# A two-layer decoder trunk: query projection in 12 tiles, rope rows moved by DMA, cumulated steps and first scan later

## The chip, the cores and the metric

The program runs on one core of a Trainium2 chip. The metric is the device time of one execution in microseconds; the median of three runs of the kernel before is 1911.82 us (1910.69 to 1912.57). The engines are named as the profile names them: PE (TensorE matmuls; PEld its weight loads), DVE (VectorE), ACT (ScalarE), POOL (GpSimd) and SP (SyncE, which issues DMAs). Each engine works through its own queue in order; semaphores join the queues.

## What is computed

Two decoder layers over 512 positions of width 1024, in float32. Each has a mixer with a Mamba-2 scan (SSD) of 16 heads in 4 groups next to a latent attention of 16 heads, a cross attention into 256 memory tokens and a gated MLP. The part that the change touches, cut from the reference:

```python
proj = h @ w_in[i]
z, xbc, dt_raw, c_q, c_kv, k_rope = jnp.split(proj, IN_SPLITS, axis=-1)
dt = jax.nn.softplus(dt_raw + dt_bias[i])
a_cs = jnp.cumsum(dt * a)                          # per chunk of 128, for the scan
q = (rmsnorm(c_q, q_norm) @ w_uq).reshape(b, s, MLA_HEADS, QK_NOPE + QK_ROPE)
q_nope = q[..., :QK_NOPE]                          # 64 wide
q_pe = apply_rope(q[..., QK_NOPE:], cos, sin)      # 32 wide: t1*cos - t2*sin, t2*cos + t1*sin
k_pe = apply_rope(k_rope, cos, sin)
sc = q_nope @ k_nope.T + q_pe @ k_pe.T             # then mask, softmax, times v
```

## The kernel before

Activations lie transposed, 128 channels by 512 positions to a tile. A float32 product is made of three matmuls (mm3, L168 to L170): both operands are split into a rounded part and a rest, and high times high, low times high, and high times low are summed in PSUM. Weights arrive by SP's queue into two raw buffers (wraw, L99); ACT writes the rounded part (whi, L107) and POOL, for some tiles DVE, the rest (wlo, L108), each into one of three buffers. So a load waits until the split of the tile two loads ago is done, and a split waits until PE has used the tile three splits ago. PSUM has 8 banks.

The order on PE is that of the program text; a scheduler orders the other engines' queues. A layer starts with the latent tiles of the input projection (query, key and value latents, key rope, dt). Then a loop interleaves generators: `projections` gives 24 input projection tiles of 24 matmuls, six for each scan group (the convolution of the first four in a group is L480 to L491, done by DVE and ACT), then `attention_head`, then `attention` with its 16 heads. In each step of that loop the lead `front`, the side work `memory` and the scans `ssd` go one step further.

`front` rotates the key's rope part (L433 to L436), makes 1/rms of both latents (the transposes of L263 and the columns by L265 to L273), broadcasts them by PE (L280), scales the rope tables for the queries (L442, L443), normalises and splits the key/value latent (L448 to L452), and then makes the cumulated sums of the scan. PE does these in L455 and L456 from w, which DVE ends in L428, the last of the dt chain L413 to L428; DVE copies the sums (L457), PE transposes them (L465), and a DMA takes them to DRAM, from which the scans fetch rows (R).

`ssd(g)` fetches its rows, then has a heavy step (transposes, decays on ACT and POOL), an empty one, the states (L558 on PE, then DVE and ACT), and the outputs (L578; L584 needs the states, made by L567 and L569). The scans go at positions 6g + 4 and after, position 26 left out.

A head in `attention` has parts in the order SKVAMTQ: scores, keys, values, attend, a memory key tile, transposes, and the query tile of the head two further on. `queries` makes 9 matmuls for one head: its columns of w_uq hold 64 plain rows, 32 rope rows and the same 32 with halves swapped; DVE multiplies the tile by a table of ones, cosines and sines, scaled by the query's 1/rms (L661), and ACT and DVE split it (L159, L162). After attention come 8 tiles of memory values; each of these steps ends with `mixed`, which writes operands of the output projection (split by L165).

Of the kernel before, what the change touches and what calls it, by code (L numbers as in the profile page):

```python
# [12 lines left out]
F32 = mybir.dt.float32  # L13
# [41 lines left out]


@with_exitstack
def trunk(ctx: ExitStack, tc: tile.TileContext, t: dict, out: bass.AP):
# [26 lines left out]
    MEM_AT = (3, 5, 7, 9, 11, 13, 14, 15)  # L85
    specs = []
# [120 lines left out]
    G.memset(mhalf, -0.5)  # L207

# [9 lines left out]
    csa = cp.tile([P, S], F32, name="csa")  # L218
    csb = cp.tile([P, S], F32, name="csb")
# [8 lines left out]
    def prepare():  # L228
        V.tensor_scalar(half[:, :, 0:80], small[:, :, o_cw:o_cw + 80], 0.5, None, ALU.mult)
        V.tensor_scalar(half[:, :, 80:], small[:, :, o_sn:o_sn + KD], 0.5, None, ALU.mult)  # L230

        ang, rnd, tab = unit(), unit(), unit()
# [3 lines left out]
        V.tensor_scalar(rnd, ang, 1.0 / (2 * math.pi), rc[:, 1:2], ALU.mult, ALU.add)  # L236
        V.tensor_scalar(rnd, rnd, magic, None, ALU.add)
# [6 lines left out]
        phs = cp.tile([P, 1], F32, name="phs")  # L244
        V.tensor_scalar(phs, rc[:, 1:2], 2 * math.pi, None, ALU.mult)
        V.tensor_scalar(ang, ang, phs, None, ALU.add)
        V.tensor_scalar(ang, ang, 3.1415925, -3.1415925, ALU.min, ALU.max)
        A.activation(tab, ang, AF.Sin)
        V.tensor_scalar(tab, tab, rc[:, 2:3], None, ALU.mult)
        G.memset(csa[0:64], 1.0)  # L250
        V.tensor_copy(csa[64:128], tab[64:128])
        V.tensor_copy(csb[0:64], tab[0:64])
        G.memset(csb[64:128], 1.0)
        A.activation(nega, small[:, :, o_al:o_al + HEADS], AF.Exp)
        V.tensor_scalar(nega, nega, -1.0, None, ALU.mult)
# [105 lines left out]
    for layer in range(L):  # L361

        cqh, cql, cqs = [], [], Squares()
# [11 lines left out]
        csqa, csqb = unit(), unit()  # L375

        def latent_q(i):
            acc = proj(hid, "w_in", layer, i)
            h_, l_ = unit(F32R), unit(F32R)
            split(h_, l_, acc, par(layer, "q_norm", i))  # L380
            cqs.add(acc)
            cqh.append(h_)
            cql.append(l_)
# [480 lines left out]
        for i in range(8):  # L864
# [8 lines left out]
            if i > 5:  # L873
                mixed(8 + i)
# [301 lines left out]
```

## Time and profile before

| | us |
|---|---|
| median of three runs | 1911.82 |
| profiled execution | 1910.9 |
| its span, first to last instruction | 1909.2 |
| PE busy | 1871.1 |
| DVE busy | 1030.6 |
| ACT busy | 950.8 |
| POOL busy | 886.3 |
| PE's longest single wait, at the start, L168 for ACT | 6.6 |

The span leaves out 1.7 us of the execution around the first and last instruction. A matmul is listed with the time from its start to its modelled end, so neighbours overlap; what one adds is seen by the distance of their starts. In the lists of waits a wait is put down to the work that ended it last. The granted clock is that of TensorE, 1.00 for its full rate of 2.4 GHz.

### The profile page before, as it was taken

How to read it: one execution, taken by the hardware profiler on the slowest of the kernel's cores; microseconds unless marked ns; L12 is line 12 of the kernel's file. 1: busy time of each engine (PE TensorE's matmuls, PEld its weight loads, DVE VectorE, ACT ScalarE, POOL GpSimd, SP SyncE). 2: the span in 40 equal slices, each digit the busy share in tenths (PEclk: the TensorE clock that was granted, in tenths of full speed). 3: DMA queues.
4: the chain of work that ended last, by engine and by line, in shares of the span. 5: the costliest groups of instructions: out<-in, count | busy, mean ns of one | idle time of the engine just before them, and what ended most of it. 6: DMA issues, size and time to landing. Idle time of an engine off the chain costs nothing.

```text
span 1909.2 us, 24928 instructions
## 1 busy us (share of the span) xinstructions
PE 1871.1 (98%) x9264; PEld 1574.3 (82%) x9264; DVE 1030.6 (54%) x1967; ACT 950.8 (50%) x1694; POOL 886.3 (46%) x563
## 2 busy tenths in 40 slices
PE   8899999999999999999999999999999999999998
PEld 6788889978888888888887887898788888888887
DVE  6777788843343555541137767887334445555312
ACT  5466588843345444433335557887333544444321
POOL 4436455555416444433354454555553354444232
PEclk9999999999999999999999999999999999999999
DMA  5233211332213233232222332113332122222322
GB/s 167 90 119 113 81 55 54 102 111 97 90 33 109 100 100 99 91 101 93 96 95 90 133 108 75 56 61 122 100 100 84 49 100 100 100 95 94 102 91 83
DMA packets 56025, 178.47 MB, mean 93 GB/s; under 512 B 6368, under 2 KB 9312, under 8 KB 55904
## 3 DMA queue, kind: packets, MB, share of 16 engines
q1 hardware_dynamic: 49984, 166.32, 26.4%
q10 hardware_dynamic: 5920, 10.55, 1.8%
q8 instruction: 73, 1.20, 0.3%
q14 instruction: 48, 0.39, 0.1%
HBM read 174.69 MB, written 2.16 MB: 93 GB/s over the span
## 4 chain that ended last, share of the span: by engine, by line
PE 91%; DVE 4%; ACT 2%; POOL 1%; issue 1%; DMA 1%; SPq 0%; ACTq 0%; POOLq 0%; DVEq 0%
PE ps L168 28%; PE ps L170 28%; PE ps L169 28%; PE ps L723 2%; PE ps L704 2%; ACT u L548 1%; POOL wlo L108 1%; DVE u L489 1%; ACT whi L107 1%; PE ps L584 1%; PE ps L578 0%; PE ps L924 0%; PE ps L726 0%; PE ps L558 0%; POOL rstd L271 0%
## 5 line engine op out<-in xcount | busy, mean ns | idle before, releaser
L108 POOL TENSOR_TENSOR wlo<-wraw,whi 128x1024 fp32r<-128x1024 f32 (+1 forms) x290 | 679.9, 2346 | 847.8 <-ACT whi L107 827.8
L168 PE MATMUL ps<-u,whi 128*128 128x512 f32 (+1 forms) x2326 | 899.7, 387 | 9.2 <-ACT whi L107 6.6
L169 PE MATMUL ps<-u,whi 128*128 128x512 f32 (+1 forms) x2326 | 890.6, 383 | 3.8 <-DVE u L165 3.8
L170 PE MATMUL ps<-u,wlo 128*128 128x512 f32 (+1 forms) x2326 | 890.7, 383 | 1.1 <-POOL wlo L108 0.6
L107 ACT ACTIVATE whi<-wraw 128x1024 fp32r<-128x1024 f32 (+2 forms) x319 | 328.2, 1030 | 505.6 <-PE ps L169 402.8
L168 PEld LDWEIGHTS ps<-u,whi 128*128 128x128 f32 x2326 | 439.3, 189 | 93.5 <-ACT whi L107 6.9
L170 PEld LDWEIGHTS ps<-u,wlo 128*128 128x128 f32 x2326 | 439.0, 189 | 87.6 <-POOL wlo L108 1.4
L169 PEld LDWEIGHTS ps<-u,whi 128*128 128x128 f32 x2326 | 439.5, 189 | 86.4 <-DVE u L165 4.9
L162 DVE TENSOR_TENSOR u<-ps,u 128x512 fp32r<-128x512 f32 (+2 forms) x236 | 136.8, 612 | 105.1 <-ACT u L159 104.2
L159 ACT ACTIVATE u<-ps 128x512 fp32r<-128x512 f32 (+2 forms) x236 | 117.3, 540 | 120.7 <-DVE ps L1013 98.3
L1009 DVE SCALAR_TENSOR_TENSOR u<-ps,small,u 128x510 f32<-128x510 f32 (+1 forms) x176 | 131.3, 749 | 74.9 <-ACT u L1007 72.0
L299 POOL TENSOR_TENSOR u<-u,u 128x512 f32<-128x512 f32 (+1 forms) x82 | 102.4, 1249 | 57.7 <-ACT u L298 56.4
L1002 DVE TENSOR_TENSOR ps<-ps,u 128x512 f32<-128x512 f32 x88 | 61.4, 700 | 109.7 <-PE ps L170 101.5
L108 DVE TENSOR_TENSOR wlo<-wraw,whi 128x1024 fp32r<-128x1024 f32 (+1 forms) x29 | 32.5, 1120 | 140.5 <-ACT whi L107 140.4
L692 POOL TENSOR_SCALAR u<-u,rs 128x512 f32<-128x512 f32 (+3 forms) x128 | 66.5, 533 | 78.4 <-DVE rs L691 74.3
L840 DVE TENSOR_TENSOR ps<-ps,u 128x512 f32<-128x512 f32 x32 | 22.4, 700 | 102.7 <-PE ps L170 102.7
L690 ACT ACTIVATE u<-ps,nm 128x512 f32<-128x512 f32 (+3 forms) x128 | 66.2, 524 | 18.0 <-DVE nm L687 12.0
L168 PE MATMUL ps<-u,u 128*128 128x512 f32 (+1 forms) x224 | 73.3, 327 | 0.9 <-ACT u L690 0.9
L489 DVE SCALAR_TENSOR_TENSOR u<-ps,half,u 128x511 f32<-128x511 f32 (+2 forms) x96 | 71.2, 744 | 3.0 <-ACT u L487 1.9
L170 PE MATMUL ps<-u,u 128*128 128x512 f32 (+1 forms) x224 | 72.1, 322 | 0.0
L169 PE MATMUL ps<-u,u 128*128 128x512 f32 (+1 forms) x224 | 72.0, 321 | 0.0
L1007 ACT ACTIVATE u<-ps,small 128x512 f32<-128x512 f32 x88 | 66.8, 761 | 1.7 <-DVE ps L1002 1.5
(193 smaller groups left out, 1765.6 us busy)
## 6 DMA issues: line engine op xcount, KB each, us to landing
wraw<-in_w_up SPq DMA_DIRECT2D x88, 512.0 KB, 3.4
wraw<-in_w_in SPq DMA_DIRECT2D x59, 512.0 KB, 3.5
wraw<-in_w_out SPq DMA_DIRECT2D x32, 512.0 KB, 3.4
wraw<-in_w_down SPq DMA_DIRECT2D x32, 512.0 KB, 3.4
u<-scr ACTq DMA_DIRECT2D x32, 256.0 KB, 4.0
wraw<-in_w_mk SPq DMA_DIRECT2D x16, 512.0 KB, 3.4
wraw<-in_w_mv SPq DMA_DIRECT2D x16, 512.0 KB, 3.5
wraw<-in_w_mq SPq DMA_DIRECT2D x16, 512.0 KB, 3.4
```

The source lines that it names most:

```text
L107: A.activation(hi[:, c], raw[:, c], AF.Copy)
L108: eng.tensor_tensor(lo[:, c], raw[:, c], hi[:, c].bitcast(F32), ALU.subtract)
L159: A.activation(hi, src, AF.Copy)
L162: (leng or V).tensor_tensor(lo, src, hi.bitcast(F32), ALU.subtract)
L168: T.matmul(o, lh, rh, start=start, stop=False)
L169: T.matmul(o, lh, rl, start=False, stop=False)
L170: T.matmul(o, ll, rh, start=False, stop=stop)
L299: (eng or G).tensor_tensor(self.acc, self.acc, sq, ALU.add)
L489: V.scalar_tensor_tensor(r_[:, d:], acc[:, :S - d], cw(3 - d), r_[:, d:], ALU.mult, ALU.add)
L692: G.tensor_scalar(p_[:, :n], p_[:, :n], rs[:, i:i + 1], 1.0, ALU.mult, ALU.mult)
L1007: A.activation(y, acc, AF.Identity, scale=fw(2), bias=par(layer, "ffn_b", ch))
L1009: V.scalar_tensor_tensor(y[:, d:], acc[:, :S - d], fw(2 - d), y[:, d:], ALU.mult, ALU.add)
```

## The change

The query projection is regrouped. Of 12 tiles a layer (`UQ`), four hold only rope rows, 32 for each of four heads, and eight hold the plain rows of two heads, 64 and 64. `query_rope` multiplies a rope tile by cosines and by sines and splits both products. `query_pair` copies and splits each half of its tile into the operand of its head, and 8 DMAs on SP's queue put the 32-row pieces of the products beside them (64 KB each, 128 of them over both layers). The key's rope tile is made in the same layout, so that the sum of both products comes out in the scores. The query's norm moves from the tables to the latent, before the projection.

```diff
+UQ = (-1, 0, 1, -1, 2, 3, -1, 4, 5, -1, 6, 7)
+    UQ_AT = (0, 1, 2, 4, 5, 6, 8, 9, 10, 12)
-        for nm, i, n in (("w_uv", 0, 1024), ("w_uk", 0, 1024), ("w_uq", 0, 768)):
+        for nm, i, n in (("w_uv", 0, 1024), ("w_uq", 0, 768), ("w_uk", 0, 1024)):
...
-                elif part == "Q" and h % 2 == 0 and h + 2 < HEADS:
-                    plan("w_uq", layer, h // 2 + 1, 768)
+                elif part == "Q" and h in UQ_AT[::2]:
+                    plan("w_uq", layer, UQ_AT.index(h) // 2 + 1, 768)
...
         def front():
-            kro, ksh = unit(), unit()
-            V.tensor_tensor(kro[64:128], dtk[64:128], csa[64:128], ALU.mult)
-            A.copy(ksh[64:96], kro[96:128])
-            V.tensor_tensor(kpe[64:96], kro[64:96], ksh[64:96], ALU.add)
-            A.copy(kpe[0:32], kpe[64:96])
             rq = rstd_cols(cqs.acc, QL, rx)
             yield
             rk = rstd_cols(cks.acc, KVL, rx)
+            if layer == 0:
+                rope_tables()
+            kro, krs, ksh = unit(), unit(), unit()
+            lo_, hi_ = slice(64, 96), slice(96, 128)
+            V.tensor_tensor(kro[lo_], dtk[lo_], csc[lo_], ALU.mult)
+            V.scalar_tensor_tensor(kro[hi_], dtk[hi_], rc[hi_, 1:2], css[hi_], ALU.mult, ALU.mult)
+            V.tensor_tensor(krs[lo_], dtk[lo_], css[lo_], ALU.mult)
+            V.scalar_tensor_tensor(krs[hi_], dtk[hi_], rc[hi_, 2:3], csc[hi_], ALU.mult, ALU.mult)
...
             pq = bcast(rq)
-            V.tensor_tensor(csqa, pq, csa, ALU.mult)
-            V.tensor_tensor(csqb, pq, csb, ALU.mult)
+            for i in range(3):
+                V.scalar_tensor_tensor(cqr[i], cqr[i], par(layer, "q_norm", i), pq, ALU.mult, ALU.mult)
+                h_, l_ = unit(F32R), unit(F32R)
+                split(h_, l_, cqr[i])
...
+            yield
             pa = bank()
             T.matmul(pa[:, :N64], triu, w, start=True, stop=True)
...
+        def query_rope(i):
+            acc, sn = query_tile(i), bank()
+            V.tensor_tensor(sn, acc, css, ALU.mult)
+            V.tensor_tensor(acc, acc, csc, ALU.mult)
+            qpe[0] = []
+            for src in (acc, sn):
+                h_, l_ = unit(F32R), unit(F32R)
+                split(h_, l_, src)
+                qpe[0].append((h_, l_))
+        def query_pair(i, pr):
+            acc = query_tile(i)
+            for j in range(2):
+                qh, ql = unit(F32R), unit(F32R)
+                rows, r0, s0 = slice(64 * j, 64 * j + 64), 64 - 64 * j, 32 * ((2 * pr + j) % 4)
+                A.activation(qh[rows], acc[rows], AF.Copy)
+                V.tensor_tensor(ql[rows], acc[rows], qh[rows].bitcast(F32), ALU.subtract)
+                for c in range(2):
+                    for dst, src in zip((qh, ql), qpe[0][c]):
+                        nc.sync.dma_start(dst[r0 + 32 * c:r0 + 32 * c + 32].bitcast(F32),
+                                          src[s0:s0 + 32].bitcast(F32))
+                qq[2 * pr + j] = qh, ql
```

The rest moves steps. The rope tables of layer 0 were built among the latent tiles and are built in `front` now. The cumulated steps come one input projection tile later (the added `yield`). The scans start at positions 5, 10, 16 and 21 without a gap; their states come directly after the heavy step and the empty step after the states. `mixed` is called two steps earlier, the first two calls at heads 14 and 15.

```diff
-            yield
-            yield
+            yield
             sw = unit(shape=(P, 2, 256))
...
+            yield
             yield
             yds = [bank(), bank()]
...
+        START = (5, 10, 16, 21)
-                if pos >= 6 * g + 4 and pos != 6 * NG + 2:
+                if pos >= START[g]:
...
+                if h + 2 >= HEADS:
+                    mixed(h + 2 - HEADS)
...
-            mixed(i)
-            if i > 5:
-                mixed(8 + i)
-        ra = rstd_cols(atts.acc, DM)
+            if i == 6:
+                ra = rstd_cols(atts.acc, DM)
+            mixed(i + 2 if i < 6 else i + 8)
```

First place, PE in the front of layer 1, before: the broadcast of the key latent's 1/rms (L280), the cumulated matmuls (L455, L456) and the first matmuls of the next tile.

```order
L170 MATMUL ps_8855<-u_8445,wlo_8806 128x512
L280 MATMUL ps_8888<-ident,rstd_8800 128x128 x4
L455 MATMUL ps_8905<-dt_1669_8457,triu 128x64
L456 MATMUL ps_8905<-dt_1669_8457,ones 128x64
L168 MATMUL ps_8920<-u_7788,whi_8851 128x512
```

The same place after: the cumulated matmuls are L470 and L471 now, and the last matmuls of a further tile (ps_8963) stand ahead of them.

```order
L173 MATMUL ps_8963<-u_8487,whi_8903 128x512
L174 MATMUL ps_8963<-u_8486,wlo_8904 128x512
L470 MATMUL ps_8996<-dt_1680_8498,triu 128x64
L471 MATMUL ps_8996<-dt_1680_8498,ones 128x64
L172 MATMUL ps_9011<-u_7829,whi_8959 128x512
```

So one input projection tile has moved ahead of the cumulated matmuls; the transposes of their sums (L465, now L480) follow one tile after them in both.

Second place, DVE at the same point, before: the copy of the cumulated sums (L457) with what stands ahead of it, from the end of the dt chain.

```order
L480 TENSOR_TENSOR ps_8809<-ps_8809,u_8657 128x512
L428 TENSOR_TENSOR dt_1669_8457<-dt_8458,nega 128x64
L442 TENSOR_TENSOR u_8466<-ps_8842,csa 128x512
L443 TENSOR_TENSOR u_8467<-ps_8842,csb 128x512
L489 SCALAR_TENSOR_TENSOR u_8834<-ps_8809,half,u_8834 128x511
L489 SCALAR_TENSOR_TENSOR u_8834<-ps_8809,half,u_8834 128x510
L489 SCALAR_TENSOR_TENSOR u_8834<-ps_8809,half,u_8834 128x509
L491 SCALAR_TENSOR_TENSOR u_8834<-ps_8809,u_8834 128x512
L480 TENSOR_TENSOR ps_8855<-ps_8855,u_8657 128x512
L457 COPY acs_8459<-ps_8905 128x64
```

After, the last rows ahead of that copy, now L472 (L453 normalises the query latent, L462 the key/value latent, L166 is a split, L495 to L506 the convolution).

```order
L495 TENSOR_TENSOR ps_8907<-ps_8907,u_8690 128x512
L506 SCALAR_TENSOR_TENSOR u_8873<-ps_8848,u_8873 128x512
L166 TENSOR_TENSOR u_8898<-u_8609,u_8897 128x512
L462 SCALAR_TENSOR_TENSOR u_8945<-u_8645,small,ps_8940 128x512
L504 SCALAR_TENSOR_TENSOR u_8932<-ps_8907,half,u_8932 128x511
L495 TENSOR_TENSOR ps_8963<-ps_8963,u_8690 128x512
L504 SCALAR_TENSOR_TENSOR u_8932<-ps_8907,half,u_8932 128x510
L166 TENSOR_TENSOR u_8948<-u_8945,u_8947 128x512
L504 SCALAR_TENSOR_TENSOR u_8932<-ps_8907,half,u_8932 128x509
L462 SCALAR_TENSOR_TENSOR u_8951<-u_8730,small,ps_8940 128x512
L472 COPY acs_8500<-ps_8996 128x64
```

Between L428 and the copy stood 7 rows before, all shown above; after, 21 rows stand between them, nine of which (L453, L462 and L166) normalise and split the two latents.

Third place, SP's queue in layer 0 where attention starts, before.

```order
L99 DMA wraw_2058<-in_w_uv 128x1024
L99 DMA wraw_2075<-in_w_uq 128x768
L99 DMA wraw_2141<-in_w_uq 128x768
L99 DMA wraw_2213<-in_w_mk 128x1024
L99 DMA wraw_2461<-in_w_uq 128x768
```

After: the first head's four rope transfers (u_2155 and u_2156 are its rounded part and rest) and the first of the second head's.

```order
L103 DMA wraw_2089<-in_w_uv 128x1024
L103 DMA wraw_2128<-in_w_uq 128x768
L103 DMA wraw_2171<-in_w_uq 128x768
L103 DMA wraw_2243<-in_w_mk 128x1024
L700 DMA u_2155<-u_2108 32x512
L700 DMA u_2156<-u_2109 32x512
L700 DMA u_2155<-u_2112 32x512
L700 DMA u_2156<-u_2113 32x512
L700 DMA u_2163<-u_2108 32x512
```

The transfers stand behind the load of w_mk, which takes the raw buffer of the w_uq load two rows ahead of it.

## Rows read from the trace of the kernel before

**Rows 1.** The page, part 1: busy us, share of the span, instructions.

```profile
PE 1871.1 (98%) x9264; PEld 1574.3 (82%) x9264; DVE 1030.6 (54%) x1967; ACT 950.8 (50%) x1694; POOL 886.3 (46%) x563
```

**Rows 2.** What PE waited for: us in total, times, longest.

```profile
PE ps L169 <- DVE u L165: 3.8, 2, 1.9
...
PE ps L584 <- DVE u L569: 2.1, 3, 1.0
...
PE ps L584 <- ACT u L567: 1.7, 2, 0.9
```

**Rows 3.** Stretches: us, busy us (instructions) PE PEld DVE ACT POOL, PEclk, DMA.

```profile
650.00:700.00 50.00, 50.00 (x222) 41.45 (x221) 25.91 (x36) 21.10 (x28) 22.40 (x10) 1.00 0.30 95
...
220.00:380.00 160.00, 156.69 (x977) 139.93 (x977) 132.11 (x366) 128.87 (x315) 88.27 (x93) 1.00 0.21 67
...
70.00:76.60 6.60, 6.21 (x17) 5.09 (x18) 5.80 (x13) 2.98 (x4) 2.38 (x1) 0.50 0.17 68
...
400.80:404.40 3.60, 3.60 (x12) 2.85 (x11) 0.87 (x2) 1.12 (x2) 2.36 (x1) 0.53 0.24 94
```

**Rows 4.** Timeline of PE: start us, us, instruction, [idle before <-releaser].

```profile
51.10 0.39 PE L170 MATMUL ps<-u,wlo 128*128 128x512 f32 x1
53.62 0.66 PE L263 MATMUL ps<-ident,u 128*128 128x128 f32 x4 [2.13 <-POOL u L299]
...
70.39 0.66 PE L455 MATMUL ps<-dt,triu 128*128 128x64 f32 x2 [4.31 <-DVE dt L428]
...
79.36 0.27 PE L465 MATMUL ps<-ident,acs 128*64 128x128 f32 x1
...
399.52 0.50 PE L169 MATMUL ps<-u,whi 128*128 128x512 f32 x1 [1.88 <-DVE u L165]
...
998.29 0.39 PE L170 MATMUL ps<-u,wlo 128*128 128x512 f32 x1
...
1013.17 0.41 PE L455 MATMUL ps<-dt,triu 128*128 128x64 f32 x2 [2.22 <-DVE dt L428]
...
1019.18 0.27 PE L465 MATMUL ps<-ident,acs 128*64 128x128 f32 x1
```

**Rows 5.** Timeline of POOL and DVE in the fronts, same columns.

```profile
66.30 2.34 POOL L108 TENSOR_TENSOR wlo<-wraw,whi 128x1024 fp32r<-128x1024 f32 x1 [1.75 <-ACT whi L107]
...
66.58 2.13 DVE L426 TENSOR_TENSOR dt<-dt,dt 128x64 f32<-128x64 f32 x1
...
73.90 2.38 POOL L108 TENSOR_TENSOR wlo<-wraw,whi 128x1024 fp32r<-128x1024 f32 x1 [5.26 <-ACT whi L107]
...
74.22 0.74 DVE L448 SCALAR_TENSOR_TENSOR u<-u,small,ps 128x512 f32<-128x512 f32 x1
...
1002.20 0.69 DVE L480 TENSOR_TENSOR ps<-ps,u 128x512 f32<-128x512 f32 x1
```

**Rows 6.** Groups by shape: count, busy us, mean ns, idle before and releaser.

```profile
L159 ACT ACTIVATE u<-ps 128x512 fp32r<-128x512 f32 x156 | 91.0, 596 | 120.4 <-DVE ps L1013 98.3 <-PE ps L170 9.9 <-DVE ps L661 5.9
...
L489 DVE SCALAR_TENSOR_TENSOR u<-ps,half,u 128x511 f32<-128x511 f32 x32 | 23.8, 745 | 2.2 <-ACT u L487 1.9
```

**Rows 7.** The rope tables: DVE timeline row, and ACT's group for its table.

```profile
43.92 2.15 DVE L243 SCALAR_TENSOR_TENSOR u<-u,u 128x512 f32<-128x512 f32 x3
...
L248 ACT ACT_TABLE_LOAD x1 | 1.3, 1283 | 0.0
```

**Rows 8.** Timeline of ACT, POOL and SP's queue around a w_uq split.

```profile
209.66 0.84 ACT L107 ACTIVATE whi<-wraw 128x768 fp32r<-128x768 f32 x1 [3.89 <-PE ps L169]
...
210.59 1.83 POOL L108 TENSOR_TENSOR wlo<-wraw,whi 128x768 fp32r<-128x768 f32 x1 [2.82 <-ACT whi L107]
...
212.44 0.33 SPq L99 DMA_DIRECT2D wraw<-in_w_uq  x1
```

**Rows 9.** DMA issues: count, KB each, median us from issue to landing.

```profile
wraw<-in_w_mk SPq DMA_DIRECT2D x16, 512.0 KB, 3.4
...
scr<-acsT ACTq DMA_DIRECT2D x2, 32.0 KB, 1.8
```

More of the change, by code (lines that the diff above doesn't have):

```diff
@@ L207, in trunk @@
     G.memset(mhalf, -0.5)
+    quart = cp.tile([P, 1], F32, name="quart")
+    G.memset(quart, math.pi / 2)
     half = cp.tile([P, L, 5 * 16 + KD], F32, name="half")
@@ L217, in trunk @@
     G.memset(vf[:, :, 1], 0.0)
-    csa = cp.tile([P, S], F32, name="csa")
-    csb = cp.tile([P, S], F32, name="csb")
+    csc = cp.tile([P, S], F32, name="csc")
+    css = cp.tile([P, S], F32, name="css")
     def load_rest():
@@ L243, in prepare @@
             V.scalar_tensor_tensor(ang, rnd, -cc, ang, ALU.mult, ALU.add)
-        phs = cp.tile([P, 1], F32, name="phs")
-        V.tensor_scalar(phs, rc[:, 1:2], 2 * math.pi, None, ALU.mult)
-        V.tensor_scalar(ang, ang, phs, None, ALU.add)
         V.tensor_scalar(ang, ang, 3.1415925, -3.1415925, ALU.min, ALU.max)
[L248 to L255, printed above, removed]
+        A.activation(css, ang, AF.Sin)
+        A.activation(ang, ang, AF.Abs)
+        A.activation(csc, ang, AF.Sin, scale=-1.0, bias=quart)
     def rstd_cols(acc, n, pre=None, nt=NT):
@@ L361, in trunk @@
     for layer in range(L):
[L363 removed]
+        cqr, cqh, cql, cqs = [], [], [], Squares()
         ckr, ckh, ckl, cks = [], [], [], Squares()
@@ L374, in trunk @@
         kpe = unit()
-        csqa, csqb = unit(), unit()
         def latent_q(i):
             acc = proj(hid, "w_in", layer, i)
-            h_, l_ = unit(F32R), unit(F32R)
-            split(h_, l_, acc, par(layer, "q_norm", i))
+            r_ = unit()
+            A.copy(r_, acc)
             cqs.add(acc)
-            cqh.append(h_)
-            cql.append(l_)
+            cqr.append(r_)
         def latent_kv(i):
@@ L604, in key_tiles @@
                     kh_, kl_ = d[nm] = (unit(F32R), unit(F32R))
[L605 to L608 removed]
+                    rr = slice(r0, r0 + 64)
+                    A.copy(kh_[rr], kpe[rr])
+                    V.tensor_tensor(kl_[rr], kpe[rr], kh_[rr].bitcast(F32), ALU.subtract)
                 kk.append(d)
@@ L651, in trunk, with query_tile @@
         qq = {}
-        def queries(h):
-            if h % 2 == 0:
-                uq[0] = weights("w_uq", layer, h // 2)
+        qpe = {}
+        def query_tile(i):
+            if i % 2 == 0:
+                uq[0] = weights("w_uq", layer, i // 2)
             uqh, uql = uq[0]
@@ L658, in queries @@
             for k in range(3):
-                o = (3 * (h % 2) + k) * P
+                o = (3 * (i % 2) + k) * P
                 mm3(acc, uqh[:, o:o + P], uql[:, o:o + P], cqh[k], cql[k], k == 0, k == 2)
-            V.tensor_tensor(acc, acc, csqb if h % 2 else csqa, ALU.mult)
-            qh, ql = unit(F32R), unit(F32R)
-            split(qh, ql, acc)
-            qq[h] = qh, ql
+            return acc
+        def query_rope(i):
[19 more added lines that the diff above has]
+                qq[2 * pr + j] = qh, ql
+        def queries(h):
+            if h in UQ_AT:
+                i = UQ_AT.index(h) + 2
+                if UQ[i] < 0:
+                    query_rope(i)
+                else:
+                    query_pair(i, UQ[i])
         pp = {}
@@ L784, in attention @@
                         mem_key(MEM_AT.index(h))
-                    elif part == "Q" and h + 2 < HEADS:
-                        queries(h + 2)
+                    elif part == "Q":
+                        queries(h)
                 if h < 2:
@@ L1104, in _layout @@
     nope, pe = uq[..., :64], uq[..., 64:]
-    full = np.empty((L, QL, HEADS, P), uq.dtype)
-    full[:, :, 0::2] = np.concatenate([nope, pe, pe[..., swap]], -1)[:, :, 0::2]
-    full[:, :, 1::2] = np.concatenate([pe, pe[..., swap], nope], -1)[:, :, 1::2]
-    full = full.reshape(L, 3, P, 8, 2, P).transpose(0, 3, 2, 4, 1, 5)
-    r["w_uq"] = full.reshape(L, 8, P, 768)
+    nope, pe = nope.reshape(L, QL, 8, P), pe.reshape(L, QL, 4, P)
+    tiles, t = [], 0
+    for u in UQ:
+        tiles.append(pe[:, :, t] if u < 0 else nope[:, :, u])
+        t += u < 0
+    full = np.stack(tiles, axis=2).reshape(L, 3, P, 6, 2, P).transpose(0, 3, 2, 4, 1, 5)
+    r["w_uq"] = full.reshape(L, 6, P, 768)
     ukv = f["w_ukv"].reshape(L, 2, P, HEADS, 2, 64)
@@ L1150, in _layout @@
     rc = np.zeros((P, 3), np.float32)
-    for b in (0, 64):
-        for j in range(64):
-            rc[b + j, 0] = inv[j % 16]
-            rc[b + j, 1] = 0.25 if j < 32 else 0.0
-            rc[b + j, 2] = 1.0 if j < 32 or j >= 48 else -1.0
+    for j in range(P):
+        rc[j, 0] = inv[j % 16]
+        rc[j, 1] = -1.0 if j % 32 < 16 else 1.0
+        rc[j, 2] = -rc[j, 1]
     r["ropec"] = rc
```

23 lines of the change are left out of this document (14 added, 9 removed).

## Prediction, written before the change was run

> **What bounds the kernel now.** I read the busy share of each engine first, then what PE waits for, then stretches, then single instructions. PE is busy for 98% of the span [rows 1]: time is saved by fewer matmuls or fewer PE waits, and lost by new PE waits or by TensorE's clock. The list of waits [rows 2] holds the few whose removal could count. A matmul's own row (387 ns in the groups of the page) is not its price, because matmuls overlap: 222 of them start in 50 us of full work [rows 3], 0.225 us each, and single rows stand 0.227 us apart. I price a 128x512 matmul at 0.227 us. The third thing to see is the granted clock: after PE's idle of 4.31 us [rows 4] it stood at 0.50 from 70.0 to 76.6 us [rows 3], the lower level of 1.2 GHz; after the idles of 2.13 and 2.22 us it stayed at the higher level; after one of 1.88 us it fell again (0.53 from 400.8 to 404.4). The price: from L455 to L465 took 8.97 us in layer 0 (70.39 to 79.36) and 6.01 in layer 1 (1013.17 to 1019.18) [rows 4], so one such episode costs 2.96 us; the one at 401 us cost about half of 3.6, 1.7.
>
> The sum is made against the profiled execution: 1909.2 us of span and 1.7 around it, 1910.9, 0.9 below the median of 1911.82. Only a difference of more than about 0.2% (3.8 us) can be told from none.
>
> **Matmuls removed.** Before, 16 query tiles a layer of 9 matmuls; after, 12. That is 4 x 9 x 2 = 72 fewer, and nothing else on PE changes in count. All lie in or just ahead of attention, where PE is busy for 156.69 of 160 us [rows 3]: 72 x 0.227 = **-16.3 us**, if no other engine becomes the limit there (rival 3). The 16 DVE and 16 ACT passes that scaled and split the query tiles are replaced by about as many of the same width, so I cost them at nothing; DVE (132.1 of 160) and ACT (128.9) hide them.
>
> **Front of the layer.** I count T from the end of the input projection tile ahead of L263: 51.33 us in layer 0, 998.52 in layer 1 (last matmul plus a step) [rows 4]. The moved cumulated steps remove the wait for L428: PE reaches them only after three further tiles, T = 17.4, while DVE does the dt chain ahead of the rope tables and is through with it at about T = 8. So 4.31 and 2.22 go, and the 2.13 ahead of L263, which came from DVE's backlog of rope tables, goes too.
>
> What is late next is the transposes of the cumulated sums (L465, now L480): they need the copy of the sums to SBUF (L457, now L472), and in DVE's order that copy stands behind more work than before. PE could be there at T = 4 x 5.45 (tiles of 24 matmuls) + 1.6 of small matmuls = 23.4. When is DVE?
>
> Layer 1: the convolution multiply of the tile at T = 0 starts at 1002.20 [rows 5], T = 3.7, and the queue ahead of it is all but the same after. From there to the copy stand 31 instructions of 512 columns, by the rows of 0.69 to 0.74 [rows 5, 6] 31 x 0.69 = 21.4, and 13 narrow ones of about 0.13. Successive ones overlap by some 0.05 us, -1.5; waits for POOL's rstd and for ACT's parts I put at 2.4. That is T = 28. On top come holds by POOL: an instruction that reads SBUF alone and starts inside a POOL L108 pass ends only with it, 2.13 in place of 0.2 (66.58 inside 66.30) [rows 5], whereas one with a PSUM operand is not held (74.22, 0.74, inside 73.90). The new products of the key's rope, the splits of the query latent and the dt chain are of the first kind, the three latent products of the second. Six POOL passes start in that time; I take two holds of 1.9, T = 32 (bounds 28 and 39).
>
> Layer 0: after the dt chain (T = 5.5) 23 wide ones, 15.9; the rope tables, now inside this queue, 5.1, of which 2.15 are the three subtractions [rows 7]; ten narrow, 1.3; overlap -1.1; the wait for Sin and Abs on ACT with a 1.28 us table load [rows 7] and for rstd 3.5: T = 30.2, with two holds 34 (bounds 30 and 40).
>
> Before, PE passed the transposes at T = 28.0 in layer 0 and 20.7 in layer 1; they now stand one tile of 5.45 later, so the same work would be there at 33.5 and 26.1. Layer 0 changes by +0.5 and layer 1 by +5.9. PE then idles for 10.6 and 8.6 us, longer than the 4.31 after which the clock fell; I add 2.96 in each (in layer 0 the old episode is already inside the 28.0). Front: **+12.3 us**, bounds -1 (no hold, no half clock) and +25 (six holds in each layer).
>
> **First scores.** Head 0 can't start its scores until four L700 transfers have put the rope rows beside its rows. They stand on SP behind a load of w_mk, and that load waits for a buffer: for POOL's split of the second w_uq tile, which waits for ACT's rounding, which waits for a rounded-weight buffer that PE frees with the last matmul of the first pair's tile. The same chain is in the trace: ACT 0.84 at 209.66, POOL 1.83 at 210.59, SP's issue at 212.44 [rows 8]. From the tile's end: 0.84 + 1.83 + five issues of 0.33 + a landing of 1.8, the row of the 32 KB store [rows 9], = 6.1 us. Landing behind the 3.4 us of the w_mk load gives the same. PE has 12 value matmuls to cover it, 2.7 us. So PE waits 3.4 at least, 4.6 with a backlog on ACT; I take 4.0 a layer and, since an idle of that length lies among those after which the clock fell and didn't, half of the 1.7 episode. **+9.7 us** for two layers, bounds 0 and +16. The transfers of the other pairs are issued almost a head ahead (some 8 us) and are hidden; without that cover each pair would cost up to the same 4.
>
> The Trainium skill (DMA: Bandwidth & Descriptors, section Bandwidth) speaks against such transfers: it asks for 1 MiB and more, and its table has 0.95 us for 64 KB. If four ran one after another at that estimate, 3.8 would stand for the four issues of 1.3, +2.5 a layer. No run here shows 64 KB yet.
>
> **Scans and tail of attention.** With the states right behind the heavy step the empty step lies behind them, so the waits of L584 go: 2.1 + 1.7 [rows 2], **-3.8**. The operands of the output projection (mixed) are written two tiles sooner than before, which takes away the 1.88 at 399.52 [rows 4], its like in layer 1 and two short ones (4.0 in all), and the 1.7 of half clock behind it: **-5.7**. Their cover is over 7 us of value matmuls.
>
> **Sum:** -16.3 + 12.3 + 9.7 - 3.8 - 5.7 = -3.8, that is 1907.1, say 1907.
>
> **Rivals.**
> 1. *DVE isn't that late* (faster). No holds: T = 30.2 and 28, 3.8 and 4 less; the transfers land at their best, 1.2 less, and no clock falls there, 1.7: 1907 - 10.7 = 1896; without the front's half clock in one layer, 1893. For it: holds hit where chance puts them, and DVE's queue is short of PSUM-free work for long pieces. Against it: in the stretch before, holds were there in both layers.
> 2. *The hold decides* (slower). The front's copy L472 lies behind 4 to 5 held instructions in place of two: T = 40 and 38, +6 each: 1907 + 12 = 1919. It decides from T = 38.3 and 36.3 on, where the sum passes +0.2%. The hold is the one of [rows 5]. For it: the new SBUF-only work stands in just this queue, and each POOL pass of 2.4 us can catch one. Against it: one POOL pass a tile, while PE stands still no new weights are freed, so POOL runs dry.
> 3. *The heads become bound by ACT*. ACT has 128.9 us in 160 [rows 3], so of at most 10 us of PE for a head 8.1. Heads 3, 7, 11 and 13 have no query tile after the change: 8.0 of PE, and of ACT 8.1 less one pass of 0.6 [rows 6], 94%, with the copies of other heads still to come. If it tips over there and in the heads with a rope tile, half of the 16.3 comes back as waits: 1915. Against it: buffers even out neighbouring heads.
> 4. *The four transfers run one after another*, each with its landing of 1.8: 7.2 for the 3.1 of the sum, +4.1 a layer: 1915. Against it: SP's issues of 0.33 don't wait for landings. The Trainium skill's 0.95 (the page above) would make it 1912.
>
> **How the numbers follow.** Forecast 0.37, alone 1900 to 1914; rival 1 0.25; rival 2 0.19; rival 3 0.12; rival 4 0.07. Faster by over 0.2% means below 1908.0: all of rival 1, and somewhat over half of the forecast, 0.21: 0.46. Slower means above 1915.6: most of rival 2, 0.17, a part of 3 and 4, 0.07, and 0.02 of the forecast: 0.26. The rest, 0.28, is no change. Range 1892 to 1921: it leaves out the case in which nothing waits in front (about 1886) and holds of both layers at their bound.
>
> **What the profile after would show.** The matmul count falls by 72. The waits for L428 and for L569 and the one at 399.5 are gone. A wait of L480 for DVE L472 stands near the top with 8 to 11 us in two pieces, and the granted clock at 0.5 behind it: steps of the front. A wait of the scores for a DMA of L700, 3 to 5 us twice: the first scores. If L480 waits under 4 us, rival 1 holds; if over 12, rival 2; if PE's share between the heads drops and ACT is named, rival 3. The prediction is wrong altogether if DVE's order isn't what sets L472, or if L700's transfers delay the weights behind them on SP.

## The result: 1924.88 us, 0.7% slower

The changed kernel takes 1924.88 us (median of six runs, 1922.81 to 1926.28) against 1911.41 us of the kernel before in the same runs: a ratio of 1.0071, 95% interval 1.0058 to 1.0083. The prediction said 1907, 1892 to 1921. The profiled execution has a span of 1924.2 us, 15.0 more than before.

First view, what PE waited for in the changed kernel (us in total, times, longest us), to be read against [rows 2]:

```profile
PE ps L769 <- DVE u L166: 7.6, 8, 1.5
PE ps L480 <- DVE acs L472: 7.2, 2, 4.1
...
PE ps L172 <- DMA u<-u: 6.2, 3, 5.2
PE ps L172 <- DVE u L643: 5.7, 3, 5.0
PE ps L282 <- DVE rstd L275: 4.9, 2, 2.4
PE ps L174 <- POOL wlo L112: 2.7, 3, 2.1
```

The waits for L428, for the states (L584, now L599) and the one at 399.52 are gone, as forecast. In their place stand L480 (the transposes of the sums), the first scores (one wait of 5.2 named for the transfer, one of 5.0 named for L643, a split of the values) and, on top, one that the sum had at nothing: L769, the attend part of the heads. In layer 1 the last transfer that the first of these matmuls needs and L643 ended within 0.02 us of each other, at 1187.57. In e5 and e6, where this code is unchanged, the waits of both layers are named for the transfer; e5's row:

```profile
PE ps L172 <- DMA u<-u: 10.6, 3, 5.2
```

PE's busy time on the page is 1868.1 us, only 3.0 less than the 1871.1 of [rows 1], although 72 matmuls are gone. Most of the rest of the 16.3 is the clock: ahead of the end of the program it stood at 1.2 GHz in eight pieces, 34 us in all, in 30 of which PE was busy, against two pieces and 10 us before. At half rate the 20 us more of busy time hold work that takes 10 at the full one. A view of stretches after each kind of wait (us, busy us and instructions of PE, PEld, DVE, ACT, POOL, then the granted clock, DMA share, GB/s), layer 0's first scores and layer 1's L282 and L480:

```profile
237.10:243.90 6.80, 4.93 (x15) 4.39 (x16) 3.16 (x11) 2.52 (x8) 1.13 (x2) 0.50 0.40 95
...
1018.00:1023.00 5.00, 4.69 (x16) 3.85 (x17) 4.75 (x9) 1.86 (x3) 0.14 (x1) 0.66 0.31 107
1035.00:1040.00 5.00, 4.00 (x12) 3.19 (x13) 5.00 (x10) 3.21 (x6) 1.84 (x1) 0.66 0.29 102
```

The table puts the 15.0 us in their places. Its stages run between rows that both kernels have: the dt transposes (L411), the first scan's transposes (L510, now L525), the first and the last attend matmuls (L723, now L769). One input projection tile (5.45 us) has moved across the border of the second and third stage, and is taken out here.

| stage | before, us | after, us | difference | the sum said |
|---|---|---|---|---|
| start to the dt transposes | 45.0 | 48.2 | +3.2 | 0 |
| front, layer 0 | 45.4 | 50.2 | -0.7 | +3.5 |
| scans and first scores, layer 0 | 158.7 | 158.9 | +5.7 | +3 |
| heads, layer 0 | 131.8 | 133.3 | +1.5 | -8.2 |
| tail and rest of layer 0 | 611.4 | 607.0 | -4.4 | -4 |
| front, layer 1 | 38.0 | 51.0 | +7.5 | +8.8 |
| scans and first scores, layer 1 | 159.6 | 157.6 | +3.4 | +3 |
| heads, layer 1 | 131.8 | 132.6 | +0.8 | -8.2 |
| tail and rest of layer 1, to the end of the span | 587.6 | 585.5 | -2.1 | -2 |

The heads alone miss the sum by 18.7 us. That is the whole error; the others miss by +3.2 (start), -5.5 (fronts) and some +3 (scores), and nearly cancel.

The heads in both kernels, the same view of stretches, before and then after:

```profile
249.00:380.80 131.80, 130.93 (x825) 118.59 (x826) 108.26 (x301) 109.40 (x265) 74.51 (x80) 1.00 0.22 73
```

```profile
257.30:390.50 133.20, 126.90 (x791) 113.29 (x790) 108.53 (x300) 110.10 (x267) 71.19 (x78) 0.99 0.30 90
```

PE has 34 matmul records less and is busy for 4 us less, and the stretch is longer. ACT (109.4 and 110.1) and DVE (108.3 and 108.5) do the same work as before, at 82 to 83% of the stretch: on average neither is full. Most of what they wait for inside these heads is each other (changed kernel, first DVE's waits, then ACT's):

```profile
DVE rs L737 <- ACT u L736: 10.5, 27, 1.0
DVE u L166 <- ACT u L163: 3.0, 4, 1.3
DVE u L779 <- ACT u L778: 2.9, 7, 0.4
```

```profile
ACT f L757 <- DVE u L166: 5.2, 6, 1.4
ACT u L736 <- DVE nm L733: 4.4, 7, 1.5
```

The average hides where the tiles are missing. In layer 0, from the attend part in head 3 to the one in head 4, PE took 7.6 us instead of 9.7, from 7 to 8 and from 11 to 12 it took 7.9 and 7.6 instead of 9.2 each. So most of the tile's time did come off there. ACT is busy for 94% of each of the three, and it was for 89, 95 and 90% of them before the change already. The three before, then after:

```profile
258.68:268.36 9.68, 9.68 (x68) 9.04 (x67) 7.65 (x20) 8.61 (x20) 5.19 (x6) 1.00 0.14 42
293.55:302.80 9.25, 9.25 (x65) 8.65 (x64) 7.96 (x25) 8.80 (x21) 6.03 (x7) 1.00 0.13 34
327.52:336.77 9.25, 9.25 (x65) 8.65 (x63) 7.52 (x22) 8.36 (x20) 6.01 (x7) 1.00 0.12 38
```

```profile
267.02:274.65 7.63, 7.63 (x60) 7.40 (x58) 6.68 (x19) 7.19 (x17) 3.72 (x5) 1.00 0.01 3
301.86:309.78 7.92, 7.34 (x56) 6.92 (x55) 7.54 (x24) 7.44 (x19) 3.97 (x6) 1.00 0.43 118
336.10:343.66 7.56, 7.33 (x56) 6.91 (x54) 6.55 (x20) 7.13 (x17) 3.67 (x5) 1.00 0.11 26
```

The waits of L769 then stand at heads 4, 8 and 12. Ahead of those at heads 4 and 8 one engine had next to no time left: in the 6 us before PE goes on, DVE is busy for 5.81 at head 4, and ACT for 5.82 at head 8. At head 12 ACT is as busy ahead of the first two of three short waits, not ahead of the last.

```profile
270.58:276.58 6.00, 4.50 (x34) 4.06 (x32) 5.81 (x15) 5.11 (x12) 4.70 (x5) 1.00 0.02 8
303.78:309.78 6.00, 5.42 (x43) 5.09 (x42) 5.62 (x19) 5.82 (x15) 3.65 (x5) 1.00 0.47 138
```

### The profile page after: what moved, and what is told of

Same layout as the page of the kernel before. It is cut to its first block, busy times and chain, and to the rows that moved or that the text cites. A ratio compares the mean times of both kernels' runs of the same rounds, so it can differ in the third digit from the quotient of the medians.

```text
span 1924.2 us, 25132 instructions
## 1 busy us (share of the span) xinstructions
PE 1868.1 (97%) x9192; PEld 1566.9 (81%) x9192; DVE 1048.7 (54%) x1967; ACT 959.2 (50%) x1712; POOL 880.6 (46%) x558
## 4 chain that ended last, share of the span: by engine, by line
PE 86%; DVE 6%; ACT 3%; issue 2%; POOL 2%; DMA 1%; SPq 0%; ACTq 0%; POOLq 0%; DVEq 0%
PE ps L172 27%; PE ps L174 27%; PE ps L173 27%; POOL wlo L112 1%; PE ps L750 1%; PE ps L769 1%; ACT u L736 1%; DVE u L166 1%; PE ps L593 1%; PE ps L599 1%; DVE ps L733 1%; DMA wraw<-in_w_in 1%; PE ps L572 1%; ACT whi L111 1%; DVE u L504 0%
## 5 line engine op out<-in xcount | busy, mean ns | idle before, releaser
L166 DVE TENSOR_TENSOR u<-ps,u 128x512 fp32r<-128x512 f32 (+2 forms) x220 | 126.8, 608 | 100.2 <-ACT u L163 97.3
L163 ACT ACTIVATE u<-ps 128x512 fp32r<-128x512 f32 (+2 forms) x220 | 107.9, 535 | 119.9 <-DVE ps L1062 98.4
L172 PE MATMUL ps<-u,u 128*128 128x512 f32 (+1 forms) x224 | 75.9, 339 | 13.2 <-DMA u<-u 6.2
L174 PE MATMUL ps<-u,u 128*128 128x512 f32 (+1 forms) x224 | 73.4, 328 | 0.0
L173 PE MATMUL ps<-u,u 128*128 128x512 f32 (+1 forms) x224 | 73.4, 328 | 0.0
L504 DVE SCALAR_TENSOR_TENSOR u<-ps,half,u 128x509 f32<-128x509 f32 (+2 forms) x96 | 70.8, 742 | 2.6 <-ACT u L502 2.1
```

Of the source, the lines that this page charges most:

```text
L163: A.activation(hi, src, AF.Copy)
L166: (leng or V).tensor_tensor(lo, src, hi.bitcast(F32), ALU.subtract)
L172: T.matmul(o, lh, rh, start=start, stop=False)
L173: T.matmul(o, lh, rl, start=False, stop=False)
L174: T.matmul(o, ll, rh, start=False, stop=stop)
L504: V.scalar_tensor_tensor(r_[:, d:], acc[:, :S - d], cw(3 - d), r_[:, d:], ALU.mult, ALU.add)
```

## The experiments

Times are medians beside runs of the kernel before, which read 1910.2 to 1911.3 us; ratios are against it.

**e4, the schedule alone.** The kernel before with the moved steps only.

```diff
-                if pos >= 6 * g + 4 and pos != 6 * NG + 2:
+                if pos >= (5, 10, 16, 21)[g]:
...
-            mixed(i)
...
+            mixed(i + 2 if i < 6 else i + 8)
```

> The kernel before with the schedule moves alone: cumulated steps one tile later, scans at 5, 10, 16 and 21 with the states directly behind the heavy step, mixed two steps sooner; the query projection, the rope tables and the key's rope as before. By the sum of the prediction: the waits for L428 (4.3 and 2.2, with 3.0 of half clock), of L584 (3.8) and the one at 399.5 (5.7) go and nothing replaces them but a short wait for the copied sums: 12 to 18 us less than the kernel before, 1894 to 1899. The other theory (the later cumulated steps are themselves what makes PE wait in front, with the query latents or without): front no better than before, and only the 7 to 9 us of the scans and the tail gained, 1903.

1897.24 us, ratio 0.9925 (0.9908 to 0.9941): 14 us faster than before, inside the first expectation. Its only long new wait, the transposes of the sums once in each layer, is not as short as that expectation had it (what PE waited for):

```profile
PE ps L466 <- DVE acs L458: 6.5, 2, 3.5
```

So the moves are worth 14 us, and the rest of the change, the regrouped projection with its rope tables, costs 28. By the stages of the table 16 of these lie in the scans and first scores (150.6 and 150.1 us here), 8 in the fronts, 3 in the start and under 2 in the heads (132.0 and 132.3 here), which gave nothing back for their missing matmuls. This kernel beats both others.

**e1, the first pair sooner.**

```diff
-        for nm, i, n in (("w_uv", 0, 1024), ("w_uq", 0, 768), ("w_uk", 0, 1024)):
+        for nm, i, n in (("w_uq", 0, 768), ("w_uv", 0, 1024), ("w_uk", 0, 1024)):
...
-            yield from values(0)
             query_rope(0)
-            yield
-            keys(0)
             query_pair(1, 0)
             yield
+            yield from values(0)
+            keys(0)
+            yield
```

> The changed kernel with the rope tile and the first pair's tile ahead of the first value tiles (their weights planned in that order): 24 value and 6 key matmuls, 6.8 us, then stand between the pair's tile and the first scores, and the first L700 transfers stand ahead of the w_mk load on SP. Theory A (PE waits at the first scores for the transfers alone, 5.2 and 5.0 us, and runs at half clock for 4.9 us behind it): both go, 2 x (5.1 + 2.4) = 15 us less than the changed kernel's 1924.9, about 1910. Theory B (the splits of the values, which end only 0.3 us before the scores start, hold the PSUM banks or DVE anyway; in layer 1 DVE L643 is named): the wait gets another name and at most 4 us are gained, 1921 or more.

1912.16 us, 12.7 less than the changed kernel, ratio 1.0008 (0.9998 to 1.0017), as theory A had it. The long waits of the first scores are gone in both layers, and the half clock behind them (scans and first scores: 158.9 to 153.0 and 157.6 to 151.8 us, 11.7 in all); one of 0.9 us for L643 is left in each. The edit does two things, transfers ahead of the load and more matmuls as cover, and doesn't tell them apart. SP's queue in the changed kernel, and then in e1, shows the order that changed (start us, us, instruction):

```profile
233.71 0.33 SPq L103 DMA_DIRECT2D wraw<-in_w_mk  x1
234.13 11.18 SPq L700 DMA_DIRECT2D u<-u  x16
```

```profile
222.85 5.03 SPq L700 DMA_DIRECT2D u<-u  x8
230.23 0.33 SPq L103 DMA_DIRECT2D wraw<-in_w_mk  x1
```

**e7, the wait filled.** 22 matmuls without a reader ahead of the first scores.

```diff
                     if part == "S":
+                        if h == 0:
+                            idle = bank()
+                            for _ in range(22):
+                                T.matmul(idle, ckh[0][:, :P], ckh[0], start=True, stop=True)
                         scores(h)
```

> The changed kernel with 22 matmuls of 128x512 added ahead of head 0's first scores in each layer (5.0 us each, into a PSUM bank that nobody reads), so that PE works through the wait for the transfers. Theory A (the wait costs twice, as idle time and as half clock behind it): the idle of 5.2 and 5.0 goes into the added matmuls, and the half clock, 6.8 us long from 237 on with PE busy at it for 4.9 us, does not come: 2.4 us less in each layer, 1920. If the clock fell for another reason than the idle time: no change, 1924 to 1925; if the added matmuls end later than the transfers land, 1 to 2 us more.

1922.09 us, ratio 1.0058 (1.0043 to 1.0073), 2.8 less; the intervals of this kernel and the changed one overlap, so the reading rests on the stages. The two stages fell by 2.3 and 2.0 us (156.6 and 155.6); the rest of the time varies with half clocks elsewhere. PE worked from 233.12 through the wait, and the clock stayed at its higher level:

```profile
233.12 5.15 PE L823 MATMUL ps<-u 128*128 128x512 f32 x22
...
238.28 0.47 PE L172 MATMUL ps<-u,u 128*128 128x512 f32 x1
```

```profile
233.00:240.00 7.00, 6.99 (x34) 5.64 (x33) 3.76 (x10) 2.61 (x6) 1.45 (x2) 1.00 0.53 152
```

So here an idle of 5 us cost a further 2 us as half clock.

**e9, fewer query matmuls in an even spread.** The kernel of e4, each query tile with 6 matmuls for 9.

```diff
-            for k in range(3):
+            for k in range(2):
```

> The kernel of e4_schedule_alone (16 query tiles a layer, as before) with 6 in place of 9 matmuls in each query tile: the third part of the query latent is left out of the sum. PE loses 3 x 12 x 0.227 = 8.2 us in the stretch of the heads (12 of the tiles lie there), just as much as the change takes away there, while the work of DVE and ACT and its place stay as they were. Theory E (before the change the heads already ran close to a second limit, the steps that DVE and ACT hand each other, at 82 to 83% busy each): the stretch of the heads stays at 129 to 132 us, and the time falls by little more than the 4 tiles outside it, 1893 to 1896 from 1897.2. Theory F (the limit comes from how the change spreads its tiles and its rope products): the heads fall to 124 to 126 us, the time to 1879 to 1883.

1890.47 us, ratio 0.9891 (0.9874 to 0.9907). The heads went from 132.0 to 129.0 us in layer 0 and from 132.3 to 128.9 in layer 1:

```profile
243.80:372.80 129.00, 125.18 (x789) 112.02 (x790) 108.04 (x302) 109.80 (x266) 74.58 (x80) 1.00 0.23 75
```

Of the 8.2 us of matmuls taken away only 3.0 and 3.4 were saved. No tile was moved, no pass of DVE or ACT changed: the other 5 us went into PE waits of up to 0.8 us and the slow starts behind them. The heads stood near a second limit already before the change. ACT is busy here for 89 to 95% of every second stretch from attend to attend, where PE doesn't wait, and most of PE's waits stand in the ones between. One of the former:

```profile
303.43:312.01 8.58, 8.58 (x61) 8.09 (x60) 6.89 (x20) 8.13 (x20) 5.46 (x7) 1.00 0.05 11
```

The time, 1890.5, lies below theory E's 1893: that number left out the 3 us a layer which the heads did give, and which lie inside its own 129 to 132; the tiles outside the heads gave 1 us in all.

**e3, no rope products for three of four tiles.**

```diff
                 if UQ[i] < 0:
-                    query_rope(i)
+                    query_tile(i)
```

> The changed kernel without the products with cosines and sines and their splits for the later three rope tiles of a layer (their matmuls stay; the pieces of the first rope tile are moved for all heads): 4 DVE and 2 ACT instructions of about 0.65 us less in heads 1, 5 and 9. Theory C (missing cover in heads 3, 7 and 11): the waits at heads 4, 8 and 12 stand two heads behind the rope tiles, so they stay; time within 3 us of 1924.9. Theory D (capacity of DVE and ACT, or the burst of the rope tile): the waits shrink by most of 4.2 us a layer, time lower by 6 or more, under 1919.

1914.88 us, ratio 1.0019 (1.0009 to 1.0028), 10.0 less, as theory D had it. The heads fell to 128.3 us in both layers, with the same PE work and 6.4 us less of DVE's:

```profile
255.60:383.90 128.30, 124.22 (x791) 111.85 (x790) 102.13 (x289) 108.23 (x263) 72.03 (x78) 1.00 0.32 95
```

The wait at head 4 stayed (1.47), those at heads 8 and 12 shrank from 1.0 and 1.7 to 0.7 and 0.5. So the products of the rope tile cost the heads some 3 to 4 us a layer, without the half clock of 1.7 that is gone in layer 0: less work for DVE and ACT at the same work for PE makes the heads shorter. Whether it is the amount of that work or that it comes in one piece, this run can't tell.

**e2, the memory key tile behind the transposes in heads without a query tile.**

```diff
+    def parts_of(h):
...
+        return ORDER if h in UQ_AT else "SKVATMQ"
...
-                for part in (FIRST if h == 0 else ORDER if h + 2 < HEADS else LAST):
+                for part in parts_of(h):
```

> The changed kernel with the memory key tile behind the transposes in the heads that have no query tile (3, 7, 11 and 13), so that 24 matmuls stand where the query tile stood before. Theory C (the heads lose the gain because without the tile PE reaches the attend part before DVE has split the transposed probabilities; waits at heads 4, 8 and 12 of 1.5, 1.0 and 1.7 us in a layer, plus refill, and half clock behind the last in layer 0): the waits of L769 fall from 8.6 us to under 3 and the time by 7 to 11, about 1916. Theory D (DVE and ACT have no capacity left over a whole head): the waits come back elsewhere in the heads, PE idle between 250 and 390 us stays within 1 us of what it was and the time within 3 us of 1924.9.

1930.42 us, ratio 1.0098 (1.0083 to 1.0113): slower by 5.5, which neither theory had. The attend at head 4 waits longer than before the edit (1.91 for 1.50), although 24 matmuls stand ahead of it now, and the transposes, which come sooner, wait too (lines are 8 higher in this kernel):

```profile
274.72 0.67 PE L777 MATMUL ps<-u,u 128*128 128x512 f32 x1 [1.91 <-DVE u L174]
...
357.05 0.41 PE L758 MATMUL ps<-ident,u 128*128 128x128 f32 x2 [1.16 <-DVE u L705]
```

The waits of the attend fell from 8.6 to 6.7 us and not under 3. That drops theory C: missing cover at one place isn't the cause; covering it uncovers the next step.

**e8, one split for a pair.** On top of e1.

```diff
+            split(q1[0], q1[1], acc)
+            for dst, src in zip(q0, q1):
+                nc.sync.dma_start(dst[0:64].bitcast(F32), src[0:64].bitcast(F32))
...
```

> The kernel of e1_pair_first with one split of 128 rows for a pair's tile in place of two of 64 rows; the rows of the first head of the pair are then taken to its own tile by two more transfers of 128 KB. DVE and ACT do 8 instructions of 0.69 and 0.59 us less in a layer. Theory D (in the heads ACT and DVE have no capacity left): the stretch of the heads shortens by 2 us or more in each layer (131.6 and 132.2 in e1_pair_first), time 1906 to 1909. Theory C (what counts is only the missing query tile as cover): heads unchanged, 1912. The longer chain of transfers could make the scores of later pairs wait; then the scores are named in the waits.

1910.99 us, ratio 1.0000 (0.9991 to 1.0010), heads 132.2 and 132.7: no gain with 4.1 us less of DVE and 2.7 less of ACT in the heads of each layer. It decides for neither theory: one score in layer 0 and two in layer 1 then waited 1.4 to 1.7 us each, about what theory D forecast as gain, and one of them is named for the longer chain of transfers. It is inconclusive.

**e5, the copy of the sums by ACT**, and **e6, the last multiply of 1/rms by POOL**, each alone on the changed kernel.

```diff
-            V.tensor_copy(acs, pa[:, :N64])
+            A.copy(acs, pa[:, :N64])
```

> The changed kernel with the copy of the cumulated sums (L472) done by ACT instead of DVE, one instruction in each layer. Theory A (DVE's queue sets when PE can transpose the sums): the waits of L480, 3.1 and 4.1 us, go, and with them the half clock that follows (1.7 us each, of 3.4 us at 1.2 GHz); the DVE work left behind is hidden: time lower by 8 to 10, about 1916. Theory B (DVE is the bound of the whole front, and PE meets it at the next step, the scan's transposes L525 or the convolved tiles): the wait moves behind and at most 3 us are gained.

```diff
-            V.tensor_tensor(r, r, pre, ALU.mult)
+            G.tensor_tensor(r, r, pre, ALU.mult)
```

> The changed kernel with the last multiply of 1/rms (L275) on POOL, directly behind POOL's own L273, instead of on DVE, where it started inside a POOL pass and took 2.29 us in place of 0.16 (1015.87). Theory A (the hold of this one instruction makes PE wait 2.4 us at L282 in each layer, with 1.7 us of half clock behind it): L282's waits fall from 4.9 us to under 1 and the front is 5 to 8 us shorter in all, unless the sums' wait at L480 takes them: DVE is not shorter by this, so L480 then waits 2 to 4 us longer in each layer and the time stays within 3 of 1924.9. I hold the second for likelier, since L472 lay at T = 31 to 32 in both layers whatever PE did before.

e5: 1921.96 us, ratio 1.0056 (1.0041 to 1.0071). The wait of L480 is gone and a like one stands at the scan, behind DVE's convolution. e6: 1923.43, ratio 1.0058 (1.0042 to 1.0075). L282 waits no more, L480 waits longer. One row of e5, then two of e6 (layer 1's second):

```profile
97.41 1.01 PE L529 MATMUL ps<-u,u 128*128 128x128 f32 x3 [5.31 <-DVE u L506]
```

```profile
83.16 0.42 PE L480 MATMUL ps<-ident,acs 128*64 128x128 f32 x1 [5.78 <-DVE acs L472]
...
1032.93 0.42 PE L480 MATMUL ps<-ident,acs 128*64 128x128 f32 x1 [6.93 <-DVE acs L472]
```

Both times lie within 3 us of the changed kernel's, as the second theory of each had it; the intervals overlap with its own, so the reading rests on the waits. In layer 0 PE meets DVE at whichever step comes next: DVE bounds the front as a whole. In layer 1 e5's front did fall from 51.0 to 46.0 us, and the two stages behind it gave part of it back (159.4 for 157.6 and 133.6 for 132.6 us, with a half clock more in the heads).

**e10 and e11, the sums ahead of the latents**, in the changed kernel (with e1's order and e12's) and in e4.

```diff
             rk = rstd_cols(cks.acc, KVL, rx)
             yield
+            pa = bank()
+            T.matmul(pa[:, :N64], triu, w, start=True, stop=True)
...
+            T.transpose(pb[:N64, :P], acs, ident)
```

> The changed kernel with e1's order of the first pair, the squares of x one tile later (so that ACT rounds the third weight tile before them), and another order in front: 1/rms of both latents, then the cumulated steps, then their transposes, and only then the key's rope with its tables, the query latents and the key/value latents, one step each. DVE's copy of the sums then stands directly behind the dt chain. If DVE's queue is what PE waits for in front: the waits of L480 and L282 (7.2 and 4.9 us) fall under 3 in all with their half clock, front 50.1 and 51.1 us to about 44, the start 1.5 us less: about 1912 - 14 = 1898. If DVE is simply too busy over the whole front, the waits come back at the scan's transposes or at the key tiles: 1906 or more.

> The kernel of e4_schedule_alone (query projection and rope as before) with the same order in front: cumulated steps and transposes ahead of the key's rope, the query tables and the key/value latents. Its waits in front are 3.5 and 3.0 us at the transposes of the sums, with 1.7 us of half clock each. If DVE's queue ahead of the copy sets them: 6 to 9 us less, 1888 to 1891. If DVE is too busy over the whole front: within 3 us of 1897.2.

1933.65 us (ratio 1.0113, 1.0098 to 1.0128) and 1909.56 (0.9994, 0.9985 to 1.0004). The gain that the first theory forecast came in neither. The second theory's bound for e10, 1906 or more, holds, but its places don't; e11 is far outside the 3 us of its second theory. In both PE then came to the cumulated matmuls before DVE's dt chain was done. In e10 the larger wait comes later, at the scan's states (L573), whose operands DVE makes in L547. The first two rows are e10's, the third e11's:

```profile
PE ps L573 <- DVE u L547: 15.9, 2, 9.2
PE ps L438 <- DVE dt L429: 10.0, 2, 7.5
```

```profile
PE ps L437 <- DVE dt L428: 15.4, 2, 7.9
```

Against this earlier place the one in the change, a tile later than before, is the better: its wait is the smaller.

**e12, the squares of x one tile later**, on top of e1.

```diff
+        latent_q(1)
+        if layer == 0:
             for k in range(KD):
                 hid.s.add(xT[k], eng=V)
-        latent_q(1)
```

> The kernel of e1_pair_first with the squares of x of layer 0 placed one tile later in the program, so that ACT rounds the third weight tile ahead of seven squares (4 us) and not behind them. If that order makes PE wait 2.0 us for POOL's rest of this tile at 23.7: the wait goes, the stretch up to the dt transposes falls from 46.1 us by 1.5 to 2, the time from 1912.2 to about 1910. If the wait comes from the arrival of the weights instead: within 1 us.

1911.93 us, ratio 1.0011 (1.0002 to 1.0021), no difference to e1 in the time. In its trace the wait of 2.0 us at 23.7 is gone and the start is 44.7 us for 46.1: the order was the cause of the wait, but a gain of 1.4 us is too small to show in these medians. The rows of the changed kernel behind it, ACT's seven squares ahead of the rounding:

```profile
16.46 3.75 ACT L300 ACTIVATE u<-xall 128x512 f32<-128x512 f32 x7
20.10 2.00 ACT L111 ACTIVATE whi<-wraw 128x1024 fp32r<-128x1024 f32 x2
```

## Why the prediction was wrong, step by step

- **The step that failed: "Matmuls removed", -16.3 us.** The price of a matmul was right, its effect was not. The sum took 0.227 us each off the end, with the condition "if no other engine becomes the limit there", and read DVE's 132 and ACT's 129 of 160 us as cover. The heads measured +1.5 and +0.8 us where -8.2 each stood. In e9 two fifths of the same cut came through with an even spread; in the change less than nothing, and e3 gave 3 to 4 us of it back by leaving rope products out. So the work of DVE and ACT sets the pace of the heads as soon as PE has less to do: e9 and e3 show that. An average over 160 us hid it: in the stretches that lose a tile ACT was busy for 89 to 95% before the change already; after it the share was 94%, just what rival 3 had worked out, and in layer 0 DVE or ACT was all but full ahead of the waits at heads 4 and 8. Rival 3 named the right place, and its sign came (PE's share of the heads fell from 99 to 95%), but with too small a price (8.2 lost; in fact 18.7, of which 1.7 is half clock) and too small a chance, and with ACT alone, where DVE's splits are named most. How much of it is load and how much the order in which the two wait for each other stays open: no run measured either by itself, and e8, which might have, is spoiled by its transfers.
- **"The front", +12.3: right in mechanism, too high.** L472 came at T = 30.9 and 31.9 (85.41 and 1035.73; T counts as in the prediction) where 34 and 32 stood, and L480 waited for it. The waits were 3.1 and 4.1 instead of 10.6 and 8.6, because PE wasn't there at T = 23.4 but at 28: it had waited 2.4 us before, at L282, for the very hold that the prediction priced, and then run at half clock. The sum counted that hold on DVE and forgot it on PE. Fronts: +6.9 in all. The dt chain, put at T = 8, ended there in layer 0 and at 16.3 in layer 1; that cost nothing, since PE came later still, but e10 and e11, with PE there sooner, ran into it. The 1886 for a front without waits doesn't follow from the terms: with PE at 23.4 in both layers they give 1882. The rows, POOL's pass and the held DVE instruction in it:

```profile
1015.80 2.34 POOL L112 TENSOR_TENSOR wlo<-wraw,whi 128x1024 fp32r<-128x1024 f32 x1
```

```profile
1015.87 2.29 DVE L275 TENSOR_TENSOR rstd<-rstd,rstd 128x4 f32<-128x4 f32 x1
```

  The Trainium skill (SBUF — State Buffer, section Who interferes with whom) has the rule: a DVE instruction with two SBUF inputs contends with a GpSimd instruction that reads SBUF, and the port pair that they share is an exclusive lock. The trace agrees: 2.29 us here for an instruction that took 0.16 at 54.61.
- **"First scores", +9.7: right in mechanism, too low.** The waits were 5.2 and 5.0 for 4.0, above the 4.6 that stood for a backlog on ACT. The half clock came both times, 2.0 to 2.3 us by e7, where 0.85 was counted. The chain through SP is in the trace: the load of w_mk was issued at 233.71, behind POOL's split, and the first transfer at 234.13. The four were issued 0.6 to 0.7 us apart, where 0.33 was counted. By e1 waits and half clock cost 11.7 us in the two stages.
- **Rival 4 fell.** Sixteen transfers were issued in 11.18 us, 0.7 each, and the median landing of all 128 is 2.0 us, so they overlap:

```profile
u<-u SPq DMA_DIRECT2D x128, 64.0 KB, 2.0
```

- **"Scans and tail", -9.5: right.** The waits are gone; the two tails gave 6.5 with what else lies in them.
- **The start, +3.2, was not looked at.** The scheduler put the rounding of the third weight tile behind seven squares on ACT; the order of the changed kernel shows that without a run. Part of it is the half clock behind the wait, which e1 with the same order didn't have (46.1 us; the runs with this start measure 46.1 to 48.2).
- **The clock was priced once in each front and half at each first scores and came oftener**: at the start, twice in each front, at both first scores and once in the heads, 34 us at half rate ahead of the end, against 10.

## What to carry to other kernels

Before matmuls are taken out of a stretch in which PE is always busy, ask what the other engines could do in less time, and ask it for the pieces that lose the matmuls, not for the average: 82% over the heads was 89 to 95% on ACT in the stretches that lost a tile, before the change already, and here two fifths of an even cut came through and nothing of an uneven one. Test it by a kernel that only drops the matmuls, before the rewrite. And test the schedule moves that come with a rewrite alone: here they were worth 14 us, and the rewrite cost twice that.

## What the hardware showed unexpectedly

The length of an idle did not decide by itself whether the clock fell. The waits of 2.44 us at L282 were followed by 1.2 GHz in both layers, and one of 2.12 at 24.06 was too; one of 2.01 at the same place in e1 was not, nor were 2.13 and 2.22 in the kernel before, while its 1.88 was [rows 3, 4]. A list of such waits with a price each is safer than a threshold.
